# Weight parts at a chosen distance modulo 512 bytes from the moving tiles, another distance for each block, and passes of 512 and 256 columns in the last layer

## The chip, the core and the metric

One core of a Trainium2 chip runs the whole program. The metric is device time in microseconds from launch to end; below it is given as the median of the runs, and once for the one execution that was profiled. The engines are TensorE (PE, with its weight loads shown apart as PEld), VectorE (DVE), ScalarE (ACT), GpSimd (POOL) and SyncE (SP), which issues the weight transfers.

## The reference, cut to what matters

A trunk of two layers on 256 tokens of width 2048, in float32. Layer 0 is a differential attention and a gated feed-forward network with a causal convolution (called FFN below), layer 1 a gated DeltaNet and a second FFN:

```python
for i in range(2):
    h = rms_norm(x, mixer_norm[i])
    x = x + (diff_attention(h, ...) if i == 0 else gated_deltanet(h, ...))
    x = x + conv_ffn(rms_norm(x, ffn_norm[i]), ffn_w_up[i], ffn_conv_w[i], ffn_conv_b[i], ffn_w_down[i])

def conv_ffn(h, w_up, conv_w, conv_b, w_down):
    u = causal_dwconv(h @ w_up, conv_w) + conv_b      # w_up is 2048 x 11008
    val, gate = jnp.split(u, 2, axis=-1)
    return (jax.nn.silu(gate) * val) @ w_down         # w_down is 5504 x 2048
```

Nearly all of the arithmetic is in products of the 256 tokens with large weight matrices.

## The kernel before, in words

Activations stand transposed: 128 channels on the partitions, 256 tokens along the free dimension. Float32 accuracy comes from splitting every operand in two parts of type float32r, a high part and a low part, and from three passes of TensorE for each product: high weights with high activations, low weights with high activations, high weights with low activations (L104, L105 and L106 in `dense`). The stationary operand of a pass is a 128x128 piece of a weight part, the moving operand 128x256 of an activation part. Such a group of three passes is called a triple below. An activation tile holds its two parts side by side, 1024 bytes each in a partition: `h` (the 16 normed input tiles), `ac` (43 tiles in an FFN, 16 in the attention) and `oc` (DeltaNet).

`dense` makes one block of 256 output channels. It walks over the contraction in chunks of four tiles of 128 rows. For each chunk `weights` (L67) fetches 512 KB by one transfer from SP into a `raw` buffer (4 buffers, L77), ACT casts it to the high part `whi` (L78) and DVE subtracts to get the low part `wlo` (L79); there are three buffers of each part. A chunk is eight triples, that is 24 passes. `dense_tok` (L115) does the same for the values of the attention and the gate `z` of the DeltaNet, with the roles exchanged: there a slice of `h` is stationary and the weight part moves, 512 columns to a pass (L125 to L127).

The blocks come in the order: 16 blocks of queries and keys, 4 of values, 8 of `w_o`; the FFN of layer 0 with 43 blocks of `w_up0` and 8 of `w_down0`; the DeltaNet, in four groups of heads, with blocks of `w_in`, `w_z` and `w_out`; the FFN of layer 1 like the first. Smaller products of attention and DeltaNet, run as generators by `tick`, stand between the passes of a block. Pads in the tiles `fcols`, `dist` and `con` shift what is allocated behind them. In the built program every moving activation tile begins 160 bytes past a multiple of 512, and every weight part 480 bytes past one, so that the moving tile lies 192 bytes behind the weights modulo 512 in every pass of `dense`. In `dense_tok` the moving weight part lies 320 bytes behind the stationary slice of `h`.

A block of `w_up` ends in PSUM in the first 256 columns of two banks; `merge` (L110) multiplies it with the norm's factor into `u` on DVE, the convolution, the activation and a split into the two parts of `ac` follow. `project` adds a block of `w_down` onto `x`.

Of the kernel before, what the change touches and what calls it, by code (L numbers as in the profile page):

```python
# [8 lines left out]
F32 = mybir.dt.float32  # L9
# [7 lines left out]
P = 128  # L17
# [3 lines left out]
EPS = 1e-6  # L21
CK = 4
LNEXP = "natural_log_exp_and_others"


class Trunk:
# [8 lines left out]
    def __init__(self, ctx, tc):  # L35
        self.tc, self.nc = tc, tc.nc
        nc = self.nc
        self.bg = deque()
        self.cp = ctx.enter_context(tc.tile_pool(name="cp", bufs=1))
        self.wp = ctx.enter_context(tc.tile_pool(name="wp", bufs=2))  # L40
        self.sp = ctx.enter_context(tc.tile_pool(name="sp", bufs=2))
        self.dps = ctx.enter_context(tc.tile_pool(name="dps", bufs=2, space=PSUM))
        self.mps = ctx.enter_context(tc.tile_pool(name="mps", bufs=4, space=PSUM))
        self.ones = self.cp.tile([P, P], F32, tag="ones", name="ones")
        nc.vector.memset(self.ones, 1.0)
        self.eps = self.cp.tile([P, 1], F32, tag="eps", name="eps")
# [7 lines left out]
        nc.scalar.preload_act_table_set(LNEXP)  # L54

    def mp(self):
# [32 lines left out]

    def dense(self, w, kt, acts, tiles=2, lead=0):  # L90

        nc = self.nc
        ps = self.banks()
        for k0, nk in self.chunks(kt, CK, lead):
            hi, lo = self.weights(w[:, k0:k0 + nk, :])
# [18 lines left out]
    def dense_tok(self, w, kt, acts):  # L114

        nc = self.nc
        ps = self.banks()
        for k0, nk in self.chunks(kt, CK // 2):
            hi, lo = self.weights(w[:, k0:k0 + nk, :])
            for k in range(nk):  # L120
# [94 lines left out]

    def add_out(self, blk, ps, done):

        x = self.x[:, 2 * blk:2 * blk + 2, :]
        self.nc.vector.tensor_tensor(x, ps[:, :, :T], x, ALU.add)
# [5 lines left out]
    def project(self, w, kt, acts, done, final=False):  # L225

        n = KD // 2
        for b in range(n - final):
            self.add_out(b, self.dense(w[b], kt, acts), done)
        if final:  # L230
            ps = self.dense(w[n - 1], kt, acts)
            for c in range(2):
                k = 2 * n - 2 + c
                self.nc.vector.tensor_tensor(self.x[:, k, :], ps[:, c, :T], self.x[:, k, :], ALU.add)
                done(k)

    def ffn(self, w_up, w_down, nj, cols_ap, done, final=False):
# [3 lines left out]
        with self.tc.tile_pool(name="fp", bufs=1) as fp:  # L241
            cols = fp.tile([P, 8 * nj + 64], F32, tag="fcols", name="fcols")[:, :8 * nj]
            cols = cols.rearrange("p (t h j) -> p t h j", t=4, h=2)
            nc.scalar.dma_start(cols, cols_ap)
            acts = []
            for j in range(nj):
                ps = self.dense(w_up[j], KD, self.h_acts)
                c = []
                u = fp.tile([P, 2, T], F32, tag="u", name="u", bufs=2)
                self.merge(ps, u)  # L250
# [8 lines left out]
                ac = fp.tile([P, 2, T], F32R, tag=f"ac{j}", name="ac")  # L259
                self.split(ac, a)  # L260
                acts.append(ac)
            self.project(w_down, nj, lambda k: acts[k], done, final)

    def attention(self, w_qk, w_v, w_o, nh, dist_ap, ident_ap, qg, kg, lvec, sub, start, done, lambda_init):

        nc, mp = self.nc, self.mp
        with self.tc.tile_pool(name="at", bufs=1) as at:
# [115 lines left out]
            for h in range(0, nh, 2):  # L383
                pv = self.dense_tok(w_v[h // 2], KD, self.h_acts)
                v = at.tile([P, 2, 2 * T], F32, tag="v", name="v", bufs=2)
# [11 lines left out]
    def gdn(self, w_gate, w_in, w_z, w_out, nb, hb, gate_ap, const_ap, hot_ap, conv_col, ng, done):  # L397
# [12 lines left out]
        with tc.tile_pool(name="gd", bufs=1) as gd:  # L410
            self.spawn(self.norm_stat())
            con = gd.tile([P, 384 + 64], F32, tag="con", name="con")[:, :384]
            nc.sync.dma_start(con, const_ap)
# [241 lines left out]
            for b in range(nb):  # L655
# [6 lines left out]
                for op, i in plan + [("v", i) for i in range(1, hb)]:  # L662
                    if op == "k":
                        hq = heads[i]
                        c = convs(lin(self.dense(w_in[hq * 2], KD, self.h_acts)), (hq, nq + hq))
                        self.spawn(keys(hq, c, cc, 2 * i, lqs))
                        if i == hb - 1:
                            self.spawn(invert(cc, lqs, inv))
                    elif op == "z":
                        gr = groups[i]  # L670
                        zt = zts[i] = gd.tile([P, 2, gv, P], F32, tag="vz", name="zt", bufs=4)
                        ps = self.dense_tok(w_z[heads[gr[0]] // 2], KD, self.h_acts)
                        for t in range(2):
                            nc.scalar.activation(zt[:, t].rearrange(flat), ps[:, t, :], AF.Silu,
                                                 scale=self.rstdc[:, t:t + 1])
                    else:
                        gi = i // gh
                        gr = groups[gi]
                        if i == gr[0]:
# [3 lines left out]
                        hq = heads[i]  # L683
                        c = convs(lin(self.dense(w_in[hq * 2 + 1], KD, self.h_acts)),
                                  (2 * nq + 2 * hq, 2 * nq + 2 * hq + 1))
# [206 lines left out]
```

## Time and profile before

| | |
|---|---|
| median of 3 runs | 2744.94 us (2742.06 to 2745.91) |
| the profiled execution | 2744.12 us, its span 2742.3 us |
| PE busy | 2728.7 us, 22352 matmuls |
| DVE busy | 1857.5 us |
| ACT busy | 1457.5 us |
| DMA | 176 GB/s mean |
| granted TensorE clock | 0.999 of the full 2.4 GHz |

The page gives busy time by engine, the chain of work that ended last, and the costliest groups. The durations of single matmuls on the page are modelled ends of a pipeline (281 ns for 256 columns, while the next one starts long before that), so what a pass costs is read from the distance between the starts of two passes, or from the number of passes in a window.

### The profile page before, as it was taken

What the parts mean: (1) busy time and instruction counts of PE and PEld (TensorE: products, weight loads), DVE (VectorE), ACT (ScalarE), POOL (GpSimd) and SP (SyncE); (2) the same over time, 40 slices, a digit from 0 to 9 for tenths busy, and PEclk for the clock granted to TensorE, in tenths of its full rate; (3) what the DMA queues carried; (4) which work ended last, traced back from release to release, by engine and by line L of the source; (5) the groups of instructions that cost most, each with busy time, mean ns of one, the idle gap of its engine ahead of it and who ended that gap; (6) DMA issues with size and microseconds to landing.
All of it is one profiled execution on the core that took longest, in us unless ns stands there. A gap on an engine that the chain in (4) does not pass through costs nothing.

```text
span 2742.3 us, 53669 instructions
## 1 busy us (share of the span) xinstructions
PE 2728.7 (100%) x22352; PEld 2656.1 (97%) x22352; DVE 1857.5 (68%) x2719; ACT 1457.5 (53%) x1994; POOL 118.4 (4%) x220
## 2 busy tenths in 40 slices
PE   8999999999999999999999999999999999999999
PEld 8998999999999999989989989989999999999999
DVE  7775667666666555688787787688676666665444
ACT  6565655555555444574764664574555555554333
POOL 0000000000000000021011011021000000000000
PEclk9999999999999999999999999999999999999999
DMA  6555555555555556545354454454455555556664
GB/s 214 169 169 169 168 189 185 186 188 188 186 186 189 185 187 187 186 155 177 122 170 140 147 172 144 155 168 157 152 187 186 186 187 188 186 186 193 191 196 151
DMA packets 135396, 481.62 MB, mean 176 GB/s; under 512 B 15344, under 2 KB 18416, under 8 KB 135152
## 3 DMA queue, kind: packets, MB, share of 16 engines
q1 hardware_dynamic: 134000, 475.57, 53.8%
q8 instruction: 175, 2.87, 0.4%
q10 hardware_dynamic: 1152, 2.61, 0.3%
q14 instruction: 69, 0.57, 0.1%
HBM read 476.03 MB, written 2.10 MB: 174 GB/s over the span
## 4 chain that ended last, share of the span: by engine, by line
PE 99%; ACT 0%; DVE 0%; DMA 0%; issue 0%; SPq 0%; DVEq 0%; ACTq 0%
PE ps L105 28%; PE ps L104 27%; PE ps L106 27%; PE ps L125 3%; PE ps L127 3%; PE ps L126 3%; PE mp L595 2%; PE mp L213 1%; PE mp L483 1%; PE mp L538 0%; PE mp L547 0%; PE mp L460 0%; PE mp L559 0%; PE mp L565 0%; PE mp L574 0%; PE mp L482 0%
## 5 line engine op out<-in xcount | busy, mean ns | idle before, releaser
L79 DVE TENSOR_TENSOR wlo<-raw,whi 128x1024 fp32r<-128x1024 f32 (+2 forms) x909 | 1108.5, 1220 | 690.1 <-ACT whi L78 685.4
L78 ACT CAST whi<-raw 128x1024 fp32r<-128x1024 f32 (+2 forms) x909 | 950.8, 1047 | 1091.3 <-PE ps L106 913.1
L104 PE MATMUL ps<-h,whi 128*128 128x256 f32 x4304 | 1208.2, 281 | 9.0 <-ACT h L139 5.3
L105 PE MATMUL ps<-h,wlo 128*128 128x256 f32 x4304 | 1209.1, 281 | 0.5 <-DVE wlo L79 0.4
L106 PE MATMUL ps<-h,whi 128*128 128x256 f32 x4304 | 1207.8, 281 | 0.0
L104 PEld LDWEIGHTS ps<-h,whi 128*128 128x128 f32 x4304 | 820.7, 191 | 11.6 <-ACT h L139 5.3
L105 PEld LDWEIGHTS ps<-h,wlo 128*128 128x128 f32 x4304 | 810.2, 188 | 4.3 <-DVE wlo L79 1.2
L106 PEld LDWEIGHTS ps<-h,whi 128*128 128x128 f32 x4304 | 809.9, 188 | 1.4
L104 PE MATMUL ps<-ac,whi 128*128 128x256 f32 x1632 | 458.4, 281 | 0.0
L105 PE MATMUL ps<-ac,wlo 128*128 128x256 f32 x1632 | 458.3, 281 | 0.0
L106 PE MATMUL ps<-ac,whi 128*128 128x256 f32 x1632 | 458.2, 281 | 0.0
L104 PEld LDWEIGHTS ps<-ac,whi 128*128 128x128 f32 x1632 | 312.2, 191 | 0.0
L105 PEld LDWEIGHTS ps<-ac,wlo 128*128 128x128 f32 x1632 | 307.2, 188 | 0.0
L106 PEld LDWEIGHTS ps<-ac,whi 128*128 128x128 f32 x1632 | 306.2, 188 | 0.0
L125 PE MATMUL ps<-whi,h 128*128 128x512 f32 x384 | 151.7, 396 | 0.0
L127 PE MATMUL ps<-whi,h 128*128 128x512 f32 x384 | 150.8, 393 | 0.0
L126 PE MATMUL ps<-wlo,h 128*128 128x512 f32 x384 | 150.6, 392 | 0.0
L104 PE MATMUL ps<-oc,whi 128*128 128x256 f32 x512 | 145.5, 284 | 0.0
L106 PE MATMUL ps<-oc,whi 128*128 128x256 f32 x512 | 145.0, 283 | 0.0
L105 PE MATMUL ps<-oc,wlo 128*128 128x256 f32 x512 | 144.8, 283 | 0.0
L194 DVE SCALAR_TENSOR_TENSOR cv<-u,fcols,cv 128x255 f32<-128x255 f32 (+1 forms) x344 | 142.8, 478 | 0.0
L112 DVE TENSOR_TENSOR u<-ps,rstd 128x512 f32<-128x512 f32 x118 | 81.4, 690 | 51.0 <-PE ps L106 50.9
(201 smaller groups left out, 2227.1 us busy)
## 6 DMA issues: line engine op xcount, KB each, us to landing
raw<-w_up SPq DMA_DIRECT2D x344, 512.0 KB, 4.3
raw<-w_down SPq DMA_DIRECT2D x160, 512.0 KB, 3.6
raw<-w_in SPq DMA_DIRECT2D x128, 512.0 KB, 4.3
raw<-w_z SPq DMA_DIRECT2D x64, 512.0 KB, 3.8
raw<-w_out SPq DMA_DIRECT2D x64, 512.0 KB, 3.6
raw<-w_qk SPq DMA_DIRECT2D x63, 512.0 KB, 4.0
raw<-w_v SPq DMA_DIRECT2D x32, 512.0 KB, 3.7
raw<-w_o SPq DMA_DIRECT2D x32, 512.0 KB, 4.3
```

The source lines that it names most:

```text
L78: nc.scalar.copy(hi, raw)
L79: nc.vector.tensor_tensor(lo, raw, hi.bitcast(F32), ALU.subtract)
L104: nc.tensor.matmul(o, hi[:, k, s], a[:, 0, :], start=first, stop=False)
L105: nc.tensor.matmul(o, lo[:, k, s], a[:, 0, :], start=False, stop=False)
L106: nc.tensor.matmul(o, hi[:, k, s], a[:, 1, :], start=False, stop=last)
L112: self.nc.vector.tensor_tensor(u, ps[:, :, :T], self.rstd.unsqueeze(1).to_broadcast([P, 2, T]), ALU.mult)
L125: nc.tensor.matmul(ps[:, c, :], ah, hi[:, k, :], start=first, stop=False)
L126: nc.tensor.matmul(ps[:, c, :], ah, lo[:, k, :], start=False, stop=False)
L127: nc.tensor.matmul(ps[:, c, :], al, hi[:, k, :], start=False, stop=last)
L194: nc.vector.scalar_tensor_tensor(out[:, j:], u[:, :T - j], taps[n - 1 - j], out[:, j:], ALU.mult, ALU.add)
L213: last = self.nc.tensor.matmul(out, self.onesr, p[:, j], start=i + j == 0, stop=i + j == n)
L595: nc.tensor.matmul(p[:, v, :], l(v), r[:, v, :], start=i == 0, stop=i == len(terms) - 1)
```

## The change

Three things change. First, `h` and the `ac` tiles of an FFN become rows of one tile each, and `weights` takes an offset `d` in floats, by which the two weight parts are moved within buffers that are 128 floats (512 bytes) longer. Each block passes an offset of its own. In the built program this gives the following distances of the moving operand behind the stationary one, in bytes modulo 512:

| blocks | before | after |
|---|---|---|
| `w_up` of both layers, block j | 192 | 16 j for j under 32, then 192 + 4 (j - 32) up to 232 |
| `w_down` of both layers, block b | 192 | 64 b |
| queries, keys and the DeltaNet's gate columns | 192 | 160 |
| `w_o` | 192 | 192 |
| `w_in`, group b of heads | 192 | 64 + 128 b |
| `w_out` | 192 | 448 |
| values, heads 0, 2, 4, 6 (512 columns) | 320 | 256, 320, 384, 448 |
| `z`, group b, pair i (512 columns) | 320 | 32 b + 16 i |

Second, `raw` has three buffers in place of four. Third, in the FFN of layer 1 (`final`, handed down as `pair`) a triple becomes two passes: the high weights with both activation parts at once, 512 columns, and the low weights with the high part, 256 columns. The sum of the two halves of a bank is then formed in `merge` by a copy on ACT and one more addition on DVE, and in `project` by a second addition on DVE.

```diff
+HP, AP = 40, 48
...
-        self.h = [self.cp.tile([P, 2, T], F32R, tag=f"h{k}", name=f"h{k}") for k in range(KD)]
+        self.hs = self.cp.tile([P, KD * 2 * T + 8], F32R, tag="h", name="h")
+        self.place(0)
...
-    def weights(self, ap):
+    def weights(self, ap, d=0):
...
-        def tile_(tag, dt, bufs):
-            t = self.wp.tile([P, CK * T], dt, tag=tag, name=tag, bufs=bufs)
-            return t[:, :nk * n].rearrange("p (k n) -> p k n", n=n)
-
-        raw, hi, lo = tile_("raw", F32, 4), tile_("whi", F32R, 3), tile_("wlo", F32R, 3)
+        def tile_(tag, dt, bufs, room=0, d=0):
+            t = self.wp.tile([P, CK * T + room], dt, tag=tag, name=tag, bufs=bufs)
+            return t[:, d:d + nk * n].rearrange("p (k n) -> p k n", n=n)
+
+        raw, hi, lo = tile_("raw", F32, 3), tile_("whi", F32R, 3, P, d), tile_("wlo", F32R, 3, P, d)
...
-                nc.tensor.matmul(o, hi[:, k, s], a[:, 0, :], start=first, stop=False)
-                nc.tensor.matmul(o, lo[:, k, s], a[:, 0, :], start=False, stop=False)
-                nc.tensor.matmul(o, hi[:, k, s], a[:, 1, :], start=False, stop=last)
+                if pair:
+                    nc.tensor.matmul(ps[:, c, :], hi[:, k, s], a, start=first, stop=False)
+                    nc.tensor.matmul(o, lo[:, k, s], a[:, 0, :], start=False, stop=last)
+                else:
+                    nc.tensor.matmul(o, hi[:, k, s], a[:, 0, :], start=first, stop=False)
+                    nc.tensor.matmul(o, lo[:, k, s], a[:, 0, :], start=False, stop=False)
+                    nc.tensor.matmul(o, hi[:, k, s], a[:, 1, :], start=False, stop=last)
...
-    def merge(self, ps, u):
+    def merge(self, ps, u, pair=False):
 
+        if pair:
+            self.nc.scalar.copy(u, ps[:, :, T:])
+            self.nc.vector.tensor_tensor(u, ps[:, :, :T], u, ALU.add)
+            self.nc.vector.tensor_tensor(u, u, self.rstd.unsqueeze(1).to_broadcast([P, 2, T]), ALU.mult)
+            return
...
+                rel = 4 * j if j < 32 else 48 + j - 32
+                ps = self.dense(w_up[j], KD, self.h_acts, pair=final, d=(HP - rel) % P)
...
+            self.project(w_down, nj, lambda k: acts[k], done, final, final, [(AP - 16 * b) % P for b in range(8)])
...
+                pv = self.dense_tok(w_v[h // 2], KD, self.h_acts, (HP + 64 + 8 * h) % P)
...
+                        c = convs(lin(self.dense(w_in[hq * 2], KD, self.h_acts, d=(HP - 16 - 32 * b) % P)), (hq, nq + hq))
...
+                        ps = self.dense_tok(w_z[heads[gr[0]] // 2], KD, self.h_acts, (HP + 8 * b + 4 * i) % P)
```

On PE the number of columns stays the same, the number of passes falls where the FFN of layer 1 begins. These are the last passes of `w_out` (`oc`) and the first of `w_up1` (`h`), before:

```order
L104 MATMUL ps_23151<-oc_22552,whi_23183 128x256
L105 MATMUL ps_23151<-oc_22552,wlo_23184 128x256
L106 MATMUL ps_23151<-oc_22552,whi_23183 128x256
L104 MATMUL ps_23229<-h0_75,whi_23231 128x256
L105 MATMUL ps_23229<-h0_75,wlo_23232 128x256
L106 MATMUL ps_23229<-h0_75,whi_23231 128x256
```

and in the changed kernel, at the same place:

```order
L120 MATMUL ps_23094<-oc_22495,whi_23126 128x256
L121 MATMUL ps_23094<-oc_22495,wlo_23127 128x256
L122 MATMUL ps_23094<-oc_22495,whi_23126 128x256
L117 MATMUL ps_23173<-h_75,whi_23175 128x512
L118 MATMUL ps_23173<-h_75,wlo_23176 128x256
```

Ahead of the boundary nothing moves; behind it each triple is two rows. The numbers behind the names count tiles.

On DVE, in the same FFN, the work on one block (u from PSUM, the convolution `cv`, the split into `ac`) stands between the subtractions `wlo` of the next blocks, before:

```order
L258 TENSOR_TENSOR cv_23501<-cv_23501,cv_23505 128x256
L79 TENSOR_TENSOR wlo_23653<-raw_23651,whi_23652 128x1024
L206 TENSOR_TENSOR ac_23511<-cv_23501,ac_23511 128x256
L79 TENSOR_TENSOR wlo_23683<-raw_23681,whi_23682 128x1024
L112 TENSOR_TENSOR u_23635<-ps_23514,rstd_23260 128x512
L79 TENSOR_TENSOR wlo_23713<-raw_23711,whi_23712 128x1024
```

and in the changed kernel:

```order
L284 TENSOR_TENSOR cv_23699<-cv_23699,cv_23703 128x256
L89 TENSOR_TENSOR wlo_23841<-raw_23839,whi_23840 128x1024
L227 TENSOR_TENSOR ac_23172<-cv_23699,ac_23172 128x256
L89 TENSOR_TENSOR wlo_23863<-raw_23861,whi_23862 128x1024
L130 TENSOR_TENSOR u_23800<-ps_23711,u_23800 128x512
L131 TENSOR_TENSOR u_23800<-u_23800,rstd_23196 128x512
L89 TENSOR_TENSOR wlo_23885<-raw_23883,whi_23884 128x1024
```

The order is the same but for one more operation on `u` ahead of a `wlo`.

## Rows read from the trace of the kernel before

**Rows 1.** The page: the span, busy time of three engines, the chain that ended last.

```profile
span 2742.3 us, 53669 instructions
PE 2728.7 (100%) x22352; PEld 2656.1 (97%) x22352; DVE 1857.5 (68%) x2719; ACT 1457.5 (53%) x1994; POOL 118.4 (4%) x220
PE 99%; ACT 0%; DVE 0%; DMA 0%; issue 0%; SPq 0%; DVEq 0%; ACTq 0%
```

**Rows 2.** Waits of PE, whole span: us in total, times, longest us.

```profile
PE ps L104 <- ACT h L139: 5.3, 1, 5.3
PE ps L104 <- ACT whi L78: 2.3, 1, 2.3
PE ps L104 <- DVE qkr L112: 1.4, 1, 1.4
PE ps L105 <- DVE wlo L79: 0.4, 1, 0.4
PE mp L704 <- DVE glin L700: 0.3, 1, 0.3
```

**Rows 3.** Windows, PE on `ps`, the two FFNs: us, busy (count), clock, DMA.

```profile
405.00:1135.00 730.00, 729.37 (x6193) 1.00 0.58 185
2008.20:2738.20 730.00, 729.59 (x6193) 1.00 0.58 186
```

**Rows 4.** Timeline of PE, a DeltaNet stretch, first and last: start us, us.

```profile
1256.75 0.28 PE L106 MATMUL ps<-h,whi 128*128 128x256 f32 x1
...
1260.37 0.28 PE L105 MATMUL ps<-h,wlo 128*128 128x256 f32 x1
```

**Rows 5.** Timeline of PE, values of the attention, first and last.

```profile
228.77 0.40 PE L125 MATMUL ps<-whi,h 128*128 128x512 f32 x1
...
233.81 0.39 PE L126 MATMUL ps<-wlo,h 128*128 128x512 f32 x1
```

**Rows 6.** Timeline of PE, two passes of `total` (L213) among passes of `dense`.

```profile
1583.87 0.28 PE L105 MATMUL ps<-h,wlo 128*128 128x256 f32 x1
1583.99 0.40 PE L213 MATMUL mp<-qp,onesr 128*128 128x512 f32 x1
1584.22 0.28 PE L106 MATMUL ps<-h,whi 128*128 128x256 f32 x1
...
1584.69 0.41 PE L213 MATMUL mp<-qp,onesr 128*128 128x512 f32 x1
1584.93 0.28 PE L104 MATMUL ps<-h,whi 128*128 128x256 f32 x1
```

**Rows 7.** The page, costliest groups: xcount | busy us, mean ns | idle before, releaser.

```profile
L79 DVE TENSOR_TENSOR wlo<-raw,whi 128x1024 fp32r<-128x1024 f32 (+2 forms) x909 | 1108.5, 1220 | 690.1 <-ACT whi L78 685.4
L78 ACT CAST whi<-raw 128x1024 fp32r<-128x1024 f32 (+2 forms) x909 | 950.8, 1047 | 1091.3 <-PE ps L106 913.1
L112 DVE TENSOR_TENSOR u<-ps,rstd 128x512 f32<-128x512 f32 x118 | 81.4, 690 | 51.0 <-PE ps L106 50.9
```

**Rows 8.** Groups of ACT and DVE by form: a copy from PSUM, an addition to `x`.

```profile
L575 ACT COPY vt<-mp 128x512 f32<-128x512 f32 x16 | 9.4, 588 | 28.9 <-PE mp L574 28.6
L219 DVE TENSOR_TENSOR x<-ps,x 128x512 f32<-128x512 f32 x55 | 37.8, 688 | 26.7 <-PE ps L106 26.5
```

**Rows 9.** Windows, busy time of DVE, then of ACT, in the last FFN.

```profile
2008.20:2738.20 730.00, 448.90 (x576) 1.00 0.58 186
2008.20:2738.20 730.00, 347.81 (x437) 1.00 0.58 186
```

**Rows 10.** The page, DMA issues: xcount, KB each, us to landing.

```profile
raw<-w_up SPq DMA_DIRECT2D x344, 512.0 KB, 4.3
```

**Rows 11.** Timeline of DVE, the end: start us, us, idle before.

```profile
2738.55 0.76 DVE L234 TENSOR_TENSOR x<-ps,x 128x256 f32<-128x256 f32 x2 [5.94 <-PE ps L106]
```

More of the change, by code (lines that the diff above doesn't have):

```diff
@@ L54, in __init__, with place, rows @@
         nc.scalar.preload_act_table_set(LNEXP)
+    def place(self, d):
+        self.h = self.rows(self.hs, KD, d)
+    def rows(self, t, n, d):
+        return [t[:, d + k * 2 * T:d + (k + 1) * 2 * T].rearrange("p (i t) -> p i t", i=2) for k in range(n)]
     def mp(self):
@@ L88, in banks, with dense @@
         return self.dps.tile([P, 2, 2 * T], F32, tag="ps", name="ps")
-    def dense(self, w, kt, acts, tiles=2, lead=0):
+    def dense(self, w, kt, acts, tiles=2, lead=0, pair=False, d=0):
         nc = self.nc
@@ L94, in dense @@
         for k0, nk in self.chunks(kt, CK, lead):
-            hi, lo = self.weights(w[:, k0:k0 + nk, :])
+            hi, lo = self.weights(w[:, k0:k0 + nk, :], d)
             steps = [(k, c) for k in range(nk) for c in range(tiles)]
@@ L118, in dense_tok @@
         for k0, nk in self.chunks(kt, CK // 2):
-            hi, lo = self.weights(w[:, k0:k0 + nk, :])
+            hi, lo = self.weights(w[:, k0:k0 + nk, :], d)
             for k in range(nk):
@@ L214, in total, with add_out @@
         return last
-    def add_out(self, blk, ps, done):
+    def add_out(self, blk, ps, done, pair=False):
         x = self.x[:, 2 * blk:2 * blk + 2, :]
-        self.nc.vector.tensor_tensor(x, ps[:, :, :T], x, ALU.add)
+        for i in range(1 + pair):
+            self.nc.vector.tensor_tensor(x, ps[:, :, i * T:(i + 1) * T], x, ALU.add)
         if done:
@@ L223, in add_out, with project @@
             self.add_squares()
-    def project(self, w, kt, acts, done, final=False):
+    def project(self, w, kt, acts, done, final=False, pair=False, ds=[0] * 8):
         n = KD // 2
[L228 to L231, printed above, removed]
+        for b in range(n):
+            ps = self.dense(w[b], kt, acts, pair=pair, d=ds[b])
+            if b < n - final:
+                self.add_out(b, ps, done, pair)
+                continue
             for c in range(2):
-                k = 2 * n - 2 + c
-                self.nc.vector.tensor_tensor(self.x[:, k, :], ps[:, c, :T], self.x[:, k, :], ALU.add)
+                k = 2 * b + c
+                for i in range(1 + pair):
+                    self.nc.vector.tensor_tensor(self.x[:, k, :], ps[:, c, i * T:(i + 1) * T], self.x[:, k, :], ALU.add)
                 done(k)
@@ L245, in ffn @@
             acts = []
+            rows = self.rows(fp.tile([P, nj * 2 * T + 8], F32R, tag="ac", name="ac"), nj, 0)
             for j in range(nj):
-                ps = self.dense(w_up[j], KD, self.h_acts)
+                rel = 4 * j if j < 32 else 48 + j - 32
+                ps = self.dense(w_up[j], KD, self.h_acts, pair=final, d=(HP - rel) % P)
                 c = []
                 u = fp.tile([P, 2, T], F32, tag="u", name="u", bufs=2)
-                self.merge(ps, u)
+                self.merge(ps, u, final)
                 for half in range(2):
@@ L258, in ffn @@
                 nc.vector.tensor_tensor(a, c[0], c[1], ALU.mult)
-                ac = fp.tile([P, 2, T], F32R, tag=f"ac{j}", name="ac")
+                ac = rows[j]
                 self.split(ac, a)
                 acts.append(ac)
-            self.project(w_down, nj, lambda k: acts[k], done, final)
+            self.project(w_down, nj, lambda k: acts[k], done, final, final, [(AP - 16 * b) % P for b in range(8)])
     def attention(self, w_qk, w_v, w_o, nh, dist_ap, ident_ap, qg, kg, lvec, sub, start, done, lambda_init):
@@ L383, in attention @@
             for h in range(0, nh, 2):
-                pv = self.dense_tok(w_v[h // 2], KD, self.h_acts)
+                pv = self.dense_tok(w_v[h // 2], KD, self.h_acts, (HP + 64 + 8 * h) % P)
                 v = at.tile([P, 2, 2 * T], F32, tag="v", name="v", bufs=2)
@@ L411, in gdn @@
             self.spawn(self.norm_stat())
-            con = gd.tile([P, 384 + 64], F32, tag="con", name="con")[:, :384]
+            con = gd.tile([P, 384], F32, tag="con", name="con")[:, :384]
             nc.sync.dma_start(con, const_ap)
@@ L683, in gdn @@
                         hq = heads[i]
-                        c = convs(lin(self.dense(w_in[hq * 2 + 1], KD, self.h_acts)),
+                        c = convs(lin(self.dense(w_in[hq * 2 + 1], KD, self.h_acts, d=(HP - 16 - 32 * b) % P)),
                                   (2 * nq + 2 * hq, 2 * nq + 2 * hq + 1))
```

4 lines of the change are left out of this document (1 added, 3 removed).

## The prediction

> **What bounds the kernel now.** I read the page first. PE is busy for the whole span and the chain that ended last runs through PE for 99% of it [rows 1], so the other engines count only where they make PE wait. The list of waits says how little that is: PE's five waits add up to under 10 us, nearly all of them at the start [rows 2]. The time is therefore the number of passes times what a pass costs, and the question is what a pass costs. The modelled 281 ns on the page don't tell it. In windows over the two FFNs 6193 passes start in 730.0 us, 117.9 ns each for 256 columns, in both of them alike [rows 3]. The granted clock is 1.00 in those windows, its upper level of 2.4 GHz, so the clock has nothing to give back. In a stretch of the DeltaNet 33 consecutive passes of the same form, with the same tiles and the same distance of 192 bytes, start in 3.62 us: 3.62/32 = 113.1 ns [rows 4]. The same pass thus has two levels, 113.1 and 117.9, and in each FFN it stays on the upper one throughout.
>
> The trace shows two other distances. In the values of the attention a part moves 320 bytes behind the stationary slice, 512 columns a pass: 23 passes, 5.04/22 = 229.1 ns, or 114.5 ns for 256 columns [rows 5]. A pass of the sums of squares of 512 columns stands 128 bytes behind the weights that are loaded under it: 0.23 and 0.24 us to the next start, 235 ns or 117.5 for 256 columns [rows 6]. Other distances are not shown in a steady stream.
>
> **The change part by part.** I count in units of 256 columns, since rows 5 show that a pass of 512 costs about as much as two of 256. The FFNs have 2 x 6192 = 12384 units (6193 in the window counts one on the edge), attention and DeltaNet 6960 in `dense` and 1152 x 2 = 2304 in `dense_tok`. That is 21648 units, so that **one nanosecond a unit is 21.6 us**, 0.8% of the time. This sets the scale of everything below.
>
> *Distance, and the 512-column pass.* For the changed kernel I take one price for all units, since the blocks run over nearly all distances. The three distances that the trace shows give 115.5 (192 bytes, midway between its two levels), 114.5 (320) and 117.5 (128); their mean is 115.8. I take 116.3, half a nanosecond more: the FFNs are runs of passes that nothing interrupts, and there rows 3 show the upper level and never the lower. The bounds are the lower level, 113.1, and 120, the dearer of the two passes in rows 6.
> - Both FFNs: (116.3 - 117.9) x 12384 = -19.8 us. In the second one this holds the effect of two passes in place of three: if the 512-column pass of rows 5 and the upper level are put together, a triple costs 229.1 + 117.9 = 347.0 in place of 353.7 ns, times 2064 triples -13.8 us, against -9.9 by the one price.
> - Attention and DeltaNet, `dense`: both levels occur there, so I set the price before at 115.5: (116.3 - 115.5) x 6960 = +5.6 us.
> - `dense_tok`: (116.3 - 114.5) x 2304 = +4.1 us.
>
> *The rule that speaks against it.* Rows 3 and 4 show one pass at two prices with addresses unchanged, so something other than the address matters as well. The Trainium skill, SBUF — State Buffer, section "Who interferes with whom", says that TensorE has two independent read ports, one for the moving operand and one for the weights, and never waits for anyone; by that rule a distance between the two can't matter. By its page TensorE: Matmul & The Clock Gate, section "Back-to-back issue gap", a pass costs its columns and 2.5 ns, 109.2 and 215.8 ns, and dropping a pass would be worth 2.5 x 2064 = 5 us; rows 3 to 5 are 4 to 13 ns above these figures, so the trace doesn't agree with them here.
>
> *Three raw buffers in place of four.* A buffer is held from the request to the end of the subtraction: 4.3 us to landing [rows 10], 1.05 us of cast, 1.22 us of subtraction [rows 7], 6.6 us. Three buffers come round in three chunks of 24 passes, 3 x 2.83 = 8.5 us. It fits, with 1.9 us to spare, and behind it two finished chunks wait in the other part buffers. The cast's idle time is ended by PE giving a buffer back, 913.1 of 1091.3 us [rows 7], so the data are there first. I cost it at nothing; if that cover were gone, PE would wait for `whi`, and the bound is one landing, 4.3 us, at the start, where fewer transfers are under way.
>
> *Merging two halves.* Per block of the last `w_up` one copy on ACT, 0.59 us by the nearest row, and one more addition on DVE, 0.69 us [rows 7, 8]: 43 x 0.59 = 25 us on an engine that is busy 348 of 730 us there, and 43 x 0.69 = 30 us on one that is busy 449 [rows 9]. Both hide under PE. Behind the longer DVE wait stands the next `wlo`; it has two chunks, 5.7 us, of lead. Per block of `w_down` one more addition of 0.69 us [rows 8], hidden likewise. Behind the last pass nothing hides it: two additions of 0.38 us become four [rows 11], and the first two run under the last passes, so between 0 and 0.8, I take +0.4 us. Moving tiles into one tile costs nothing: the order of waits on PE stays as it was.
>
> Sum: -19.8 + 5.6 + 4.1 + 0.4 = -9.7 us. The profiled execution took 2744.1 us, 0.8 below the median, which is less than the runs differ; 2744.1 - 9.7 = **2734 us**. A measurement here can tell about 0.2%, 5.5 us, from no change, so the forecast lies just outside of that.
>
> **The rivals.**
> 1. *The swept distances are dearer: slower.* The kernel before holds one distance in all blocks of `dense`. If the interference of the two reads is near its lowest there, a sweep pays the mean over all. For it: 128 bytes costs 117.5 to 120 [rows 6], the highest of the three seen, and 512 passes of `w_out` and 1536 of queries and keys go to distances not seen before in a stream (448 and 160). Against it: 320 is no dearer than 192. At 119 ns a unit the time is 2734 + 2.7 x 21.6 = 2792 us. It decides from 117.0 ns on: (117.0 - 116.3) x 21.6 = 15 us takes the forecast to 2749, 0.2% above now.
> 2. *New blocks fall on the lower level.* If each shift of the weights sets the two streams anew and they come to rest at 113.1 [rows 4], the time is 2734 - 3.2 x 21.6 = 2665 us. Against it: levels change in the trace only where other products stand between.
> 3. *The distance does nothing.* The levels stay as they are in each stage, and only the wide pass counts: -13.8 + 0.4, 2731 us, or no gain if a wide pass costs twice a narrow one on the upper level, 2744. The rule of the Trainium skill's page SBUF — State Buffer, cited above, would give this outcome.
>
> **How the numbers follow.** The forecast, a price between 115.6 and 117.0, gets 0.33, the first rival 0.35, since one side of the known distances is dearer and the price that decides is only 0.7 ns away, the second 0.14, the third 0.18. Faster by over 0.2%: 0.20 of the forecast's share, all of the second rival's, 0.13 of the third's: 0.47. Within 0.2%: 0.12 of the forecast, 0.05 of the third: 0.17. Slower: the first rival and 0.01 of the forecast: 0.36. The bounds 113.1 and 120 ns give 2665 and 2814; leaving out a tenth on either side the range is 2675 to 2805. Cases of both signs hold much of the chance; the forecast's own range, 115.6 to 117.0 ns, is 2719 to 2749.
>
> **What would show it.** The number of passes in a window over each block of `w_up` gives a price for each distance. Right: blocks between 113 and 120 ns whose mean is near 116.3, PE without new waits, in the last FFN triples of some 349 ns. Wrong by the first rival: whole blocks above 118, above all at distances under 192. By the second: all blocks at 113. By the third: the first FFN flat at 117.9. If `L104`'s successor waits for `whi` anywhere but at the start, three raw buffers are too few.

## The result and the profile after

The changed kernel takes 2757.44 us (median of 5 runs, 2752.46 to 2757.79) where the kernel before takes 2744.61 (median of 5). The ratio is 1.0044 [1.003, 1.0059]: it is slower, by 0.44%, while the forecast said faster by 0.4%. The time lies in the range, on the side of the first rival.

The page of the changed kernel, beside [rows 1]:

```profile
span 2753.9 us, 49636 instructions
PE 2738.2 (99%) x20288; PEld 2571.3 (93%) x20288; DVE 1888.1 (69%) x2771; ACT 1473.5 (54%) x2037; POOL 117.1 (4%) x220
PE 99%; DMA 0%; DVE 0%; ACT 0%; issue 0%; SPq 0%; DVEq 0%; ACTq 0%
```

There are 2064 matmuls fewer, as many as the last FFN has triples, and the span is 11.6 us longer. PE still fills it, and the chain that ended last is still PE. The waits of PE answer to [rows 2]:

```profile
PE ps L120 <- ACT h L160: 6.0, 1, 6.0
PE ps L121 <- DVE wlo L89: 2.7, 3, 1.4
PE ps L120 <- ACT whi L88: 2.1, 2, 2.0
PE mp L730 <- DVE glin L726: 0.2, 1, 0.2
```

Their sum is 11.0 us in place of 9.7, all but 2.5 us of it in the first 20 us. So no wait has come in place of another: passes cost more. Where they do is told by windows over the six stages (attention, `w_up0`, `w_down0`, DeltaNet, `w_up1`, `w_down1`), PE on `ps`: us, busy (count), clock, DMA share, GB/s. First the changed kernel, then the kernel before:

```profile
0.00:410.49 410.49, 375.35 (x2689) 1.00 0.53 176
410.49:900.13 489.64, 489.01 (x4131) 1.00 0.57 186
900.13:1140.26 240.13, 240.13 (x2067) 1.00 0.59 185
1140.26:2023.60 883.34, 756.00 (x5426) 1.00 0.47 156
2023.60:2507.38 483.78, 483.15 (x2755) 1.00 0.58 188
2507.38:2749.05 241.67, 241.67 (x1378) 1.00 0.60 186
```

```profile
0.00:405.00 405.00, 370.43 (x2689) 1.00 0.55 179
405.00:892.06 487.06, 486.43 (x4131) 1.00 0.58 187
892.06:1135.15 243.09, 243.09 (x2066) 1.00 0.58 182
1135.15:2008.20 873.05, 746.88 (x5427) 1.00 0.49 158
2008.20:2495.26 487.06, 486.65 (x4130) 1.00 0.57 187
2495.26:2738.30 243.04, 243.04 (x2066) 1.00 0.59 184
```

Line by line the differences are +5.5, +2.6, -3.0, +10.3, -3.3 and -1.4 us, and the end, from the start of the last pass on, grew from 4.1 to 4.9 us, +0.8. The granted clock is 1.00, the upper level, in every stage of both kernels. The four FFN stages together give 5.0 us back, not 19.8; attention and DeltaNet cost 15.8 us, not 9.7.

Windows from the start of one block to the start of the next give the price of each distance. Six blocks of `w_up0` of the changed kernel, at 16, 32, 64, 128, 256 and 204 bytes, then two of `w_down0`, at 0 and 64 (the counts include passes on the edges; a block is 96 passes in `w_up`, 258 in `w_down`):

```profile
422.86:434.37 11.51, 11.51 (x98) 1.00 0.54 180
434.37:445.58 11.21, 11.21 (x99) 1.00 0.57 184
456.77:468.08 11.31, 11.31 (x98) 1.00 0.58 189
502.44:513.82 11.38, 11.38 (x99) 1.00 0.57 186
593.50:605.02 11.52, 11.52 (x99) 1.00 0.56 184
809.73:820.61 10.88, 10.88 (x98) 1.00 0.62 189
900.13:931.09 30.96, 30.96 (x261) 1.00 0.59 181
931.09:960.33 29.24, 29.24 (x261) 1.00 0.61 190
```

Divided by 96 or 258 these are 119.9, 116.8, 117.8, 118.5, 120.0, 113.3, 120.0 and 113.3 ns a pass. All blocks of `w_up0` read in this way:

| distance, bytes | ns a pass in `w_up0` of the changed kernel |
|---|---|
| 0, 16, 96, 112, 144 | 119.9 to 120.0 (the first block, 0, has other products in it and takes 128.9) |
| 32, 48 | 116.7, 116.6 |
| 64, 80, 192 | 117.8, 118.1, 117.8 |
| 128, 160, 176, 208, 224, 240 | 118.3 to 118.7 |
| 256 to 496 | the values of 0 to 240 again; 256 itself 120.0 |
| 196, 200, **204**, 208, 212 (steps of 4) | 119.4, 117.7, **113.4**, 117.8, 117.8 |
| 216, 220, 224, 228, 232 | 119.1, 119.9, 118.3, 116.7, 118.6 |

So the price changes with the distance, it repeats after 256 bytes, and nearly all of a sweep in steps of 16 lies at or above the 117.8 that the kernel before pays at 192. Two things in the same trace don't fit one price for each distance. 208 bytes stands in the table twice, at 118.3 behind a block at 192 and at 117.8 behind one at 204. And the eight blocks of `w_down0`, at 0, 64, up to 448 bytes, cost 120.0, 113.3, 118.6 and 113.4, then 120.0, 113.3, 118.6 and 113.4 ns: 64, 192, 320 and 448 bytes cost 113.3 to 113.4 there and 117.8 in `w_up0`.

### The profile page after: what moved, and what is told of

It is laid out like the page before. It is cut to its first block, busy times and chain, and to the rows that moved or that the text cites. A ratio compares the mean times of both kernels' runs of the same rounds, so it can differ in the third digit from the quotient of the medians.

```text
span 2753.9 us, 49636 instructions
## 1 busy us (share of the span) xinstructions
PE 2738.2 (99%) x20288; PEld 2571.3 (93%) x20288; DVE 1888.1 (69%) x2771; ACT 1473.5 (54%) x2037; POOL 117.1 (4%) x220
## 4 chain that ended last, share of the span: by engine, by line
PE 99%; DMA 0%; DVE 0%; ACT 0%; issue 0%; SPq 0%; DVEq 0%; ACTq 0%
PE ps L121 19%; PE ps L120 19%; PE ps L122 19%; PE ps L117 17%; PE ps L118 9%; PE ps L146 3%; PE ps L148 3%; PE ps L147 3%; PE mp L621 2%; PE mp L234 1%; PE mp L509 1%; PE mp L564 0%; PE mp L573 0%; PE mp L486 0%; PE mp L585 0%; PE mp L591 0%
## 5 line engine op out<-in xcount | busy, mean ns | idle before, releaser
L120 PE MATMUL ps<-h,whi 128*128 128x256 f32 x2928 | 824.0, 282 | 8.1 <-ACT h L160 6.0
L122 PE MATMUL ps<-h,whi 128*128 128x256 f32 x2928 | 823.5, 281 | 0.0
L120 PEld LDWEIGHTS ps<-h,whi 128*128 128x128 f32 x2928 | 552.8, 189 | 10.9 <-ACT h L160 6.0
L122 PEld LDWEIGHTS ps<-h,whi 128*128 128x128 f32 x2928 | 552.2, 189 | 1.3
L117 PE MATMUL ps<-h,whi 128*128 128x512 f32 x1376 | 483.1, 395 | 0.0
L117 PEld LDWEIGHTS ps<-h,whi 128*128 128x128 f32 x1376 | 258.5, 188 | 61.2
L120 PE MATMUL ps<-ac,whi 128*128 128x256 f32 x944 | 263.7, 280 | 0.0
L122 PE MATMUL ps<-ac,whi 128*128 128x256 f32 x944 | 263.5, 279 | 0.0
L117 PE MATMUL ps<-ac,whi 128*128 128x512 f32 x688 | 241.8, 395 | 0.0
L121 PEld LDWEIGHTS ps<-ac,wlo 128*128 128x128 f32 x944 | 178.9, 190 | 0.0
L120 PEld LDWEIGHTS ps<-ac,whi 128*128 128x128 f32 x944 | 178.0, 189 | 0.0
L122 PEld LDWEIGHTS ps<-ac,whi 128*128 128x128 f32 x944 | 177.9, 189 | 0.0
L117 PEld LDWEIGHTS ps<-ac,whi 128*128 128x128 f32 x688 | 129.2, 188 | 30.6
L146 PE MATMUL ps<-whi,h 128*128 128x512 f32 x384 | 151.8, 396 | 0.0
```

What stands on the lines that cost most here:

```text
L117: nc.tensor.matmul(ps[:, c, :], hi[:, k, s], a, start=first, stop=False)
L146: nc.tensor.matmul(ps[:, c, :], ah, hi[:, k, :], start=first, stop=False)
```

## The experiments

My theory after this reading: a pass has a price for each distance, the sweep pays the mean of them, and most are dearer than what was there. The rivals: the other edits cost the time (the wide pass, three raw buffers, tiles that came to lie elsewhere), or what counts is the address and not the distance. All kernels hold the whole computation. Ratios are to the kernel before, which was run again beside each group of experiments (medians of 2743.0 to 2743.5 us). The six stages are given in the order used above.

One edit of the change is named nowhere ahead of the prediction: the pad of 64 floats in `con`, in the DeltaNet, is gone. With the 8 floats by which `h` and the `ac` tile of an FFN grew, this moves the tiles that are allocated behind them. Experiment 9 takes it back.

**1. All blocks at the old distances.** The weights lie in the new tiles, but 192 bytes from the moving tile everywhere (320 in `dense_tok`).

```diff
-                rel = 4 * j if j < 32 else 48 + j - 32
+                rel = 48
...
-            self.project(w_down, nj, lambda k: acts[k], done, final, final, [(AP - 16 * b) % P for b in range(8)])
+            self.project(w_down, nj, lambda k: acts[k], done, final, final, [(AP - 48) % P for b in range(8)])
...
-                pv = self.dense_tok(w_v[h // 2], KD, self.h_acts, (HP + 64 + 8 * h) % P)
+                pv = self.dense_tok(w_v[h // 2], KD, self.h_acts, (HP + 80) % P)
```

(Queries and keys, the gate and `w_in` get `(HP - 48) % P`, `w_z` the offset of `w_v`, `w_out` 64.)

> The changed kernel with every distance put back to what the kernel before has (192 bytes in dense, 320 in dense_tok); single tiles, three raw buffers and the two-pass triples of the last layer stay. Theory A (the loss is the distances of the blocks of attention and DeltaNet, which in the kernel before reach the lower level of 113.3 ns in part of their passes): attention ends near 405 us and the DeltaNet takes near 873 us as before, not 410 and 883; the total is within 5 us of the kernel before, since the two-pass triple at 192 bytes costs 117.5 ns a unit of 256 columns against 117.9. Theory B (three raw buffers, the merged tiles or the other order of instructions cost the 16 us there): attention and DeltaNet stay at 410 and 883 us and the total stays near 2757 us.

Measured: 2734.11 us, ratio 0.9966 [0.9953, 0.9979]; stages 406.9, 468.8, 243.1, 878.5, 487.0, 243.0. The distances alone turn slower into faster. But attention and DeltaNet came only part of the way back to 405.0 and 873.0, and `w_up0` did what nobody expected: at the same 192 bytes it ran 18.3 us shorter than before. Windows of `w_up0` and `w_up1`:

```profile
406.90:875.70 468.80, 468.17 (x4131) 1.00 0.60 194
1997.30:2484.30 487.00, 486.37 (x2754) 1.00 0.60 187
```

468.8/4128 is 113.6 ns, the lower level of [rows 4], held through 43 blocks: all behind the first, which has other products in it, cost 113.3 to 113.4.

**2. Three passes in the last FFN too.** The sweep stays, `pair` goes.

```diff
-                ps = self.dense(w_up[j], KD, self.h_acts, pair=final, d=(HP - rel) % P)
+                ps = self.dense(w_up[j], KD, self.h_acts, d=(HP - rel) % P)
...
-                self.merge(ps, u, final)
+                self.merge(ps, u)
```

> The changed kernel with three passes a triple in the last layer too; all distances as in the change. Theory A (price by distance, the same in both FFNs): the last FFN costs block by block what the first one costs in the changed kernel, 730 us in place of 725, total near 2762 us. Theory B (the wide pass costs as much as it saves; its 5 us are the sweep falling otherwise): last FFN stays near 725 us, total 2757 us.

Measured: 2758.9 us, 1.0057 [1.004, 1.0074]; the stages of the last FFN are 489.6 and 240.0 in place of 483.8 and 241.6, the same as those of the first FFN. The wide pass is worth 729.6 - 725.4 = 4.2 us in the sweep by these windows; the medians of the runs differ by 1.5 us, with ranges that meet. It is not what made the change slower.

**3. The sweep in the FFNs alone.** Attention and DeltaNet as in run 1, the FFNs as in the change.

> The changed kernel with the distances of attention and DeltaNet put back to 192 and 320 bytes; the FFNs as in the change (swept, two passes in the last). Theory A (their distances cost 16 us): attention ends near 405 us, DeltaNet takes 873 us, total 2757 - 16 = 2741 us. Theory B (buffers, tiles, order): total stays at 2757 us.

Measured: 2746.21 us, 1.0011 [1.0002, 1.0021]; 406.7, 489.6, 240.1, 880.3, 483.8, 241.6. Of the 15.8 us that attention and DeltaNet had lost, the distances make 3.8 + 3.0 = 6.8; 1.7 and 7.3 remain that they don't explain. The split has a spread: runs 1, 3, 4, 6 and 8 hold the same code there and have 406.2 to 407.5 and 878.0 to 880.3 us.

**4. The best distances of the sweep.** 204 bytes for `w_up`, 64 for `w_down`, three passes; the rest as in run 3.

```diff
-                rel = 4 * j if j < 32 else 48 + j - 32
+                rel = 51
...
-            self.project(w_down, nj, lambda k: acts[k], done, final, final, [(AP - 16 * b) % P for b in range(8)])
+            self.project(w_down, nj, lambda k: acts[k], done, final, False, [(AP - 16) % P for b in range(8)])
```

> Distances of attention and DeltaNet as before; in both FFNs three passes a triple, all blocks of w_up at 204 bytes and all of w_down at 64 bytes, the places of the sweep that showed 113.4 ns. Theory A (the distance sets the price by itself): each FFN takes 12384 passes / 2 x 113.4 ns = 702 us in place of 730, total near 2744 - 56 = 2689 us. Theory B (at such a distance two levels exist and what ran before decides): the FFNs' long runs start from another state and stay near 117.8 ns, total near 2744 us, or one FFN of each kind, 2717 us.

Measured: 2714.18 us, 0.9893 [0.9878, 0.9908]; `w_up` 468.8 twice, `w_down` 243.1 and 243.0. One half of the expectation held, the other didn't: 204 bytes gave the lower level, 64 bytes gave 117.8 ns, though the sweep has 113.3 there. In the sweep the block at 64 stood behind one at 0, here behind blocks at 204. So 64 bytes, like 192, has two levels. That the blocks ahead differ is what the next run builds on; this one alone doesn't show that they are the reason.

**5. A block at 0 ahead of those at 64,** and 204 bytes in queries, keys, gate, `w_in` and `w_out` as well.

```diff
-            self.project(w_down, nj, lambda k: acts[k], done, final, False, [(AP - 16) % P for b in range(8)])
+            self.project(w_down, nj, lambda k: acts[k], done, final, False, [AP] + [AP - 16] * 7)
```

> The kernel of e4 with two more places on the lower level: in each w_down the first block at 0 bytes and the other seven at 64 (the order in which the changed kernel came onto 113.3 ns there), and queries, keys, w_in, the gate columns and w_out at 204 bytes. Theory A (history chooses between two levels at 64 bytes; at 204 only the lower one holds): each w_down takes 258 x 120.0 + 1806 x 113.3 ns = 236 us in place of 243; attention ends near 402 us (406 in e4), the DeltaNet takes about 870 us (878); total near 2714 - 15 - 12 = 2687 us. Theory B (the level at 64 bytes is chance, and among interruptions 204 is no better than 192): 2714 us.

Measured: 2698.3 us, 0.9837 [0.982, 0.9855]; 408.8, 468.8, 235.6, 873.9, 468.8, 235.5. With the block at 0 in front, the seven others stand on the lower level: (235.6 - 31.0)/(7 x 258) = 113.3 ns, the 31.0 being the block at 0 as the sweep showed it. With 204 bytes the DeltaNet is shorter than in run 4 (878.1 to 873.9), the attention longer (406.2 to 408.8).

**6. The levels by what stands ahead.** In `w_up0` every other block lies at 204, in `w_up1` at 192; the blocks between walk through 0, 24, 48, up to 480 bytes. Three passes, attention and DeltaNet as in run 1.

```diff
-                rel = 4 * j if j < 32 else 48 + j - 32
+                rel = 6 * (j // 2) if j % 2 else 48 if final else 51
```

> Three passes everywhere, attention and DeltaNet as before. In the first w_up every even block at 204 bytes, every odd one at another distance (0 to 480 in steps of 24); in the second the same with 192 in place of 204; in each w_down every second block at 64 bytes, between blocks at 0, 32, 128 and 96. Theory A (204 has one level, 192 and 64 have two, and the block before decides): all 22 blocks at 204 cost 113.3 to 113.5 ns a pass wherever they come from; the blocks at 192 fall apart into some at 113.3 and some at 117.8, none between; the blocks at 64 likewise. Theory B (the distance alone sets the price): the blocks at 192 all cost the same. Total between 2725 and 2745 us.

Measured: 2737.9 us, 0.9982 [0.9972, 0.9993]. In `w_up1`, windows of four blocks at 192 bytes, which stand behind blocks at 0, 48, 72 and 96:

```profile
2032.01:2043.32 11.31, 11.31 (x99) 1.00 0.62 184
2077.18:2088.07 10.89, 10.89 (x99) 1.00 0.60 192
2099.38:2110.69 11.31, 11.31 (x99) 1.00 0.64 188
2122.20:2133.08 10.88, 10.88 (x98) 1.00 0.61 191
```

The form, the tiles and the distance are the same, 117.8 or 113.4 ns. Of the 22 blocks at 192 without other products in them (21 of the alternating ones, and one that the walk through the distances puts there), 13 took the lower and 9 the upper, 113.3 to 113.5 or 117.8, none lay between. In `w_down0` the block at 64 bytes is at 113.3 behind the one at 0, and those behind 32, 128 and 96 bytes are at 117.8. The part of the expectation that gave 204 bytes one level fell: 19 of its 22 blocks are at 113.3 to 113.9 and the first, which has other products in it, at 123.3, but the two behind 72 and 120 bytes are at 120.0 and 119.9. So 204 too can be held on a dear level by what ran ahead. The first of these pairs, 72 and then 204, and below it two blocks at 24 bytes, behind 204 in `w_up0` and behind 192 in `w_up1`:

```profile
485.60:496.90 11.30, 11.30 (x98) 1.00 0.64 189
496.90:508.40 11.50, 11.50 (x99) 1.00 0.65 188
440.73:452.56 11.83, 11.83 (x98) 1.00 0.59 180
2043.32:2054.68 11.36, 11.36 (x99) 1.00 0.60 186
```

24 bytes costs 123.2 ns in the one and 118.3 in the other, so it has two levels as well, and the first is the dearest block without other products in this run. The blocks at 168 bytes, behind 204 and behind 192, both cost 113.3: 204 is not the only cheap place.

Does the distance of the block ahead choose the level? Not that alone. Here are a block at 192 behind one at 176, in the changed kernel (block 12 of `w_up0`), and one at 192 behind one at 432, in `w_up1` of this run:

```profile
548.12:559.42 11.30, 11.30 (x98) 1.00 0.55 186
2435.55:2446.44 10.89, 10.89 (x98) 1.00 0.66 191
```

432 is 176 modulo 256, and yet the first block is at 117.8 and the second at 113.5. What ran ahead decides, and more of it than the last distance modulo 256. It is no chance: runs 2, 3 and 11 hold the same sequence of distances in `w_up0` as the change, and the price of each block behind the first agrees within 0.03 ns.

**7. Three raw buffers in the kernel before.**

```diff
-        raw, hi, lo = tile_("raw", F32, 4), tile_("whi", F32R, 3), tile_("wlo", F32R, 3)
+        raw, hi, lo = tile_("raw", F32, 3), tile_("whi", F32R, 3), tile_("wlo", F32R, 3)
```

> The kernel before with three raw buffers in place of four and nothing else (every address stays the same modulo 512). Theory A (three are enough, as the prediction had it): attention ends at 405 us, DeltaNet takes 873 us, total 2744 us. Theory B (the 7 us that attention and DeltaNet still lose in e1 with all distances put back come from the missing buffer): attention 407 us, DeltaNet 878 us, total 2751 us.

Measured: 2745.45 us, 1.0008 [0.9998, 1.0017]: no difference that can be told. Attention and DeltaNet are 405.6 and 874.6 us, the FFN stages 487.1, 243.1, 487.1, 243.0, those of the kernel before.

**8. Run 1 with three passes.** It separates the wide pass from the level.

> The kernel of e1 (all distances as before) with three passes a triple in the last layer too. Theory A (two levels at 192, chosen by what came before): the first FFN does as in e1, w_up 469 us, w_down 243 us; the last FFN takes either 469 or 487 us for w_up, nothing between, and 235 to 243 for w_down; with the upper level the total is that of e1, 2734 us, which would say that the two-pass triple is worth nothing against three passes on the upper level, with the lower one 2716 us. Theory B (the two-pass triple is worth 5 us by itself): last FFN 735 us, total 2739 us.

Measured: 2715.02 us, 0.9897 [0.9881, 0.9912]; `w_up1` is 468.8 in place of 487.0, all else as in run 1:

```profile
407.50:876.30 468.80, 468.17 (x4131) 1.00 0.64 194
1997.40:2466.20 468.80, 468.39 (x4131) 1.00 0.65 194
```

A triple of `w_up1` is 468.8/1376 = 340.7 ns with three passes on the lower level, and 487.0/1376 = 353.9 with a wide and a narrow one, which is what three passes cost on the upper level. In run 1 the wide pass took 235.0 ns and the narrow one 118.3.

**9. Every tile at the place it had before,** modulo 512, in the new code: single offsets of 0, no extra floats in `h` and `ac`, `con` longer by 64, three passes, three raw buffers.

```diff
-        self.hs = self.cp.tile([P, KD * 2 * T + 8], F32R, tag="h", name="h")
+        self.hs = self.cp.tile([P, KD * 2 * T], F32R, tag="h", name="h")
...
-            con = gd.tile([P, 384], F32, tag="con", name="con")[:, :384]
+            con = gd.tile([P, 384 + 64], F32, tag="con", name="con")[:, :384]
```

> The kernel of e8 (192 and 320 bytes everywhere, three passes, three raw buffers, single tiles) with the pads of the kernel before, so that every tile lies at the address modulo 512 that it has in the kernel before. Theory A (what attention and DeltaNet lost in e1 and e8 beyond the distances, 7 us, and the level on which an FFN starts, come from the places of the small tiles, whose products interrupt the stream): attention 405 to 406, DeltaNet 873 to 875 us, both w_up on the upper level again, 487 us, total 2745 us. Theory B (they come from the single tiles and the order): attention 407, DeltaNet 878, w_up 469 us each, total 2715 us as e8.

Measured: 2745.89 us, 1.0009 [1.0, 1.0019]; 404.4, 487.1, 243.1, 873.8, 487.1, 243.0. That is the kernel before, stage by stage, with `w_up0` on the upper level:

```profile
404.40:891.46 487.06, 486.43 (x4130) 1.00 0.61 187
```

The distances in `dense` and `dense_tok` are those of run 8. What differs is where the small tiles lie, whose products stand between the passes, and where `ac` and `oc` lie together with their weights. These places bring attention from 407.5 to 404.4 and DeltaNet from 878.0 to 873.8, which is 1.8 to 3.1 and 4.2 to 6.5 us against all the runs with the code of run 8 there, and put both `w_up` on the upper level, 487.1 in place of 468.8. So tiles that no pass of `w_up` reads decide here on which level its 43 blocks run; by which way isn't shown.

**10. The best of both.** Run 9 with 204 bytes for gate, `w_in`, `w_out` and `w_up`, and 0 and then seven times 64 bytes for `w_down`.

```diff
-                ps = self.dense(w_up[j], KD, self.h_acts, d=0)
+                ps = self.dense(w_up[j], KD, self.h_acts, d=125)
...
-            self.project(w_down, nj, lambda k: acts[k], done, final, False, [0] * 8)
+            self.project(w_down, nj, lambda k: acts[k], done, final, False, [48] + [32] * 7)
```

> The places of e9 with queries and keys at 192 bytes, w_in, the gate columns, w_out and both w_up at 204, the first block of each w_down at 0 and the rest at 64. Theory A: w_up 469 and w_down 236 us in both FFNs as in e5, attention 405 (409 in e5), DeltaNet 868 to 872 us (874 in e5); total 2690 us. Theory B (the places of the small tiles do not matter): attention 407, DeltaNet 874 us, total 2697 us.

Measured: **2692.14 us, 0.9817 [0.9803, 0.9832]**, the fastest version of all, 51 us under the kernel before and 65 under the change. Windows of the last five stages:

```profile
404.60:873.40 468.80, 468.17 (x4131) 1.00 0.66 194
873.40:1109.00 235.60, 235.60 (x2066) 1.00 0.65 188
1109.00:1980.50 871.50, 744.41 (x5427) 1.00 0.52 158
1980.50:2449.30 468.80, 468.39 (x4131) 1.00 0.65 194
2449.30:2684.80 235.50, 235.50 (x2066) 1.00 0.67 192
```

Against the kernel before, 51.6 us are gained in the four FFN stages and 1.5 in DeltaNet. The counts are the same: the same passes, only their places moved.

**11. Distance or address.** `h` and the weights move 32 bytes together, so each block of `w_up` keeps its distance and has other addresses.

```diff
-HP, AP = 40, 48
+HP, AP = 48, 48
...
-        self.place(0)
+        self.place(8)
```

> The changed kernel with the tile h moved by 32 bytes and the weight parts of its blocks with it: all distances of w_up as in the change, other addresses. Theory A (the distance sets the price, not the address): block for block the prices of the change, 120.0 at 0 and 16, 116.7 at 32 and 48, 118.5 at 128, in the first w_up, with 113.3 or 117.8 at 64, 192, 320 and 448. Theory B (the weights' address or the alignment of h sets it): the prices shift by two blocks, or the blocks at 64 + 128 n all fall to 113.3.

Measured: 2746.85 us, 1.0013 [1.0003, 1.0024]. The six blocks of `w_up0` shown above for the change (`w_down` has not moved here):

```profile
418.08:429.59 11.51, 11.51 (x99) 1.00 0.58 180
429.59:440.79 11.20, 11.20 (x98) 1.00 0.59 184
451.99:463.30 11.31, 11.31 (x99) 1.00 0.60 187
497.65:509.03 11.38, 11.38 (x98) 1.00 0.57 186
588.71:600.23 11.52, 11.52 (x98) 1.00 0.58 184
804.95:815.83 10.88, 10.88 (x99) 1.00 0.62 189
```

They agree within 0.01 us. In a stream of narrow passes the distance counts, and moving both tiles by 32 bytes changes nothing. In the last FFN, with wide passes, nearly all blocks agree as well, but `w_up1` at 16 bytes costs 115.6 ns for 256 columns where it cost 117.8, and `w_down1` at 64 bytes 117.8 where it cost 116.3.

Attention and DeltaNet did change, to 405.7 and 879.9 from 410.5 and 883.3. For the attention this tells nothing of the address: queries and keys (and the gate of the DeltaNet) take no offset in the code, so that their weights stayed while `h` moved, and their distance went from 160 to 192 bytes. The whole gain lies there: the start of the first query block to the start of the values took 206.6 us in the change and 201.8 here. In the DeltaNet all distances but that of the gate are those of the change, and it is 3.4 us shorter, where the change and run 2, with the same code there, agree within 0.2 us. This agrees with run 9: where small products stand between, the places of `h` and of the small tiles against each other count too.

## Why the prediction was wrong

**What bounds the kernel:** right. PE ran without new waits, so the time is the number of passes times their price.

**The price, 116.3 ns for all units: this is the step that failed.** By the same sum as in the prediction, +11.6 in place of -9.7 us is 21.3/21.6 = 1.0 ns more for a unit, 117.3. Three parts of it were mis-sized.
- *Both FFNs*, -19.8 forecast, -5.0 measured: (489.6 + 240.1 + 483.8 + 241.6)/12384 = 117.5 ns. The mean of the three distances seen was no mean over a sweep. One of them, 114.5 at 320 bytes, is half a pass of 512 columns in which the roles are exchanged [rows 5]; a stream of 256 columns at 320 bytes costs 117.8 in `w_up0` and 113.3 in `w_down0`. Another, 115.5 at 192 bytes, was the middle of two levels [rows 3, 4], and the middle is a price that no block has: in run 6 all 22 lie on the one level or the other. (The 117.9 of rows 3 holds the other products of the first block; the blocks behind it cost 117.8.) The dear end, 120, from [rows 6], bounds the sweep of the first FFN, which lies near it: the sixteen steps from 0 to 240 bytes have a mean of 118.6, and only those at 32 and 48 are clearly under 117.8.
- *The wide pass inside that term.* I priced it by the values of the attention, 229.1 ns, a triple at 347 to 349. It is 351.6 in the change (483.8 us/1376). By run 2 the wide pass is worth 4.2 us where I had 13.8, and the last FFN as a whole gained 4.7 where I had 9.9. Block by block, apart from the first, its units cost 115.6 to 121.1 ns, never the 113.3 of the cheap narrow ones. At 192 bytes it costs 235.0 and gains nothing over three passes on the upper level.
- *Attention and DeltaNet*, +9.7 forecast, +15.8 measured. The mean distance of starts of passes of `dense` that follow each other on one sum rose from 116.0 to 118.0 ns in the 2304 passes of the attention and from 115.6 to 116.9 in the 4656 of the DeltaNet, 4.6 + 6.1 = 10.7 us where I had 5.6; the 115.5 that I took for the time before was close. In the attention all of it is in the queries and keys, which went from 192 to 160 bytes, 115.3 to 118.3 ns; `w_o`, which kept 192, took 117.4 in both kernels. Passes of 512 columns rose by 0.9 ns (384 of them) and 2.2 (768), 2.1 us where I had 4.1. The other 3.0 us lie at the seams with the small products. I had put the places of the small tiles at nothing, without a reason, though the pads `fcols`, `dist` and `con` are there in the code and the change takes that of `con` away; run 9 puts 3.1 and 4.2 us on them, part of which is in the passes counted above.

**Three raw buffers at nothing:** right by run 7, within its interval (at most 0.17%, 4.7 us), and run 9, which has three as well, reproduces the stages before to 0.8 us.

**Merging, hidden:** right. Groups of the changed kernel beside [rows 7, 8], then busy time of DVE and ACT in the last FFN beside [rows 9]:

```profile
L129 ACT COPY u<-ps 128x512 f32<-128x512 f32 x43 | 24.9, 579 | 0.0
L130 DVE TENSOR_TENSOR u<-ps,u 128x512 f32<-128x512 f32 x43 | 29.4, 683 | 0.0
L131 DVE TENSOR_TENSOR u<-u,rstd 128x512 f32<-128x512 f32 x43 | 29.8, 692 | 1.5
```

```profile
2023.60:2749.00 725.40, 478.28 (x626) 1.00 0.59 187
2023.60:2749.00 725.40, 367.25 (x480) 1.00 0.59 187
```

The copy was to cost 588 and took 579 ns, the addition 690 and took 683. Both engines have some 250 us or more to spare there, and PE waits for neither. Behind the last pass the four additions cost 0.8 us more, the upper end of what I gave, where I took 0.4.

**The rivals.** The first, that the swept distances are dearer, is what happened, just past its point of decision (117.3 against 117.0 ns). Its reason was half right: the 117.8 of 192 bytes is under the mean of the sweep, but it is not near the lowest, which is 113.3, at 192 bytes too. (`w_out` makes 1536 passes, not 512: those are its triples.) The second, blocks falling on the lower level, is what runs 1, 4, 5, 8 and 10 made happen; the change has it only at 204 bytes and in some blocks of `w_down`. My argument against it, that levels change only where other products stand between, fell: in run 6 they change from block to block without any. The third fell too: the price runs from 113.3 to 120.0 ns with the distance, in run 6 to 123.2. This doesn't agree with what the Trainium skill, SBUF — State Buffer, section "Who interferes with whom", says of TensorE, that its two read ports are independent and that it never waits on anyone. That the two reads are what gets in each other's way is argued from the distance; no trace shows the reads themselves. The 109.2 and 215.8 ns that the prediction set beside rows 3 to 5 come from a formula that the Trainium skill, TensorE: Matmul & The Clock Gate, section "Back-to-back issue gap", gives for a single matmul that stands alone, so rows of a stream don't test it.

**Open:** why the price repeats with 256 bytes, and what sets the level at 192, 64, 204 and 24 bytes. Run 6 shows that what ran ahead decides it, not by which rule, nor how far back it reaches. Which of the moved tiles changes attention and DeltaNet, and the level of `w_up`, wasn't separated, and distances in steps of 4 bytes were tried only from 192 to 232.

## What to carry to other kernels

Where PE is the bound and its passes stream, count passes in a window over each block and divide: a few nanoseconds between blocks of the same form, with the clock the same and no wait, can be a layout effect, and a sweep over distances is an instrument to find the cheap one, not a setting to run with. Fix the cheapest distance, then look whether it holds in the order in which the blocks come, since a price can have two levels and what ran ahead can choose between them. When a layout changes, read the stages with many small products as well, because tiles that nobody meant to move have moved there.

## What the runs showed of the chip that I had not expected

- A pass of 256 float32r columns costs 113.3 to 120.0 ns in the first FFN of the changed kernel, at a granted clock of 1.00, by the distance of its moving operand behind the stationary one, with a period of 256 bytes; 24 bytes took 123.2 in run 6. 204 bytes is 113.4, its neighbours at 200 and 208 are 117.7 and 117.8.
- At one distance with one set of tiles it has two levels, 113.4 and 117.8 at 192 bytes, and what ran ahead selects which. A level holds for whole blocks, in run 1 for the 468.8 us of 43 blocks.
- A pass of 512 columns in a stream of the last FFN took 235.0 ns at 192 bytes, so that a triple with it cost 353.9 ns, 13.2 more than three passes on the lower level.
